# A two-layer hybrid decoder on eight cores: first transfers in the order of use, compact gate weights, the first blocks run k by k, sample tokens moved to the last tile, a scheduler that counts table loads exactly

## The chip, the cores and the metric

The kernel runs as one program on all eight cores of one Trainium2 chip, two dies of four cores. The metric is the device time in microseconds (us) of the slowest core. Each core works alone: it takes one prompt sequence of 2048 tokens and 16 sample sequences of 4 tokens, and reads all weights itself.

Runs come in two states. In the slow state the cores of one die show a lower granted TensorE clock, and the time is up to some 18% longer, whatever the kernel; such runs are left out everywhere below. The runs were made on several chips, and the chips differ by up to 0.8 per cent in fast runs too, so an experiment is always compared with runs of the kernel before on the same chip, in the same rounds.

## The reference

Each of two layers does the following (cut to what matters):

```python
hn = _rmsnorm(x, norm_in)
z  = hn @ w_in                        # 1024 -> 8 x 1024
u_a, b_a, c_a, g_a, x_b, g_b, m_a, m_b = split(z)
y_a = b_a * conv3(c_a * u_a) * silu(g_a)               # branch A
xc  = conv4(x_b) + bias                                # branch B
r   = sigmoid(xc @ blockdiag(w_r) + b_r)               # 16 blocks of 64 x 64
gi  = sigmoid(xc @ blockdiag(w_i) + b_i)
a   = exp(-8 * r * softplus(-lam))
h_t = a_t * h_(t-1) + sqrt(1 - a_t**2) * gi_t * xc_t   # a scan over time
y_b = h * silu(g_b)
x   = x + (sigmoid(m_a) * (y_a @ w_a_out) + sigmoid(m_b) * (y_b @ w_b_out)) @ w_o
x   = x + (p[l] @ w_pe) * sigmoid(_rmsnorm(x) @ w_pg)
```

A final RMSNorm follows. The prompt starts from zero states; the samples start from given convolution and recurrent states. The outputs are y and the new states of both.

## The kernel before

The 2112 tokens of a core are cut into five tiles of 424 columns (the last has 416), in two groups: tiles 0 and 1, then tiles 2, 3 and 4. For each group and layer an *A phase* makes the branches: eight units j of 128 channels, and for each tile six *blocks* of eight matmuls with weights w_A, two *gate matmuls* (the 64 x 64 blocks, two to a 128 x 128 matrix) and the elementwise work. A *B phase* merges them, with weights w_M, w_O and w_G. The B phase of one group runs interleaved with the A phase of the next; so there are five stages, and only stage 0 (A phase of two tiles) and the last (B phase of three) have TensorE work of one kind.

The order is not written by hand. The kernel states each operation with its reads, writes, a priority and an estimated duration for each engine that may do it. A list scheduler then fixes the buffers, the engine and the order of every instruction. On the chip each engine runs its list strictly in that order, waiting on semaphores where data come from another engine.

The parts (cuts marked):

```python
SETS = {"tanh": ("exp", "silu"), "exp": ("exp", "lnexp"), "silu": ("silu",), ...}
WIN, WIN_W = 45.0, 30.0
...
def schedule(self):
    ...
    for o in cand[e]:
        if o.prio > head[o.stream] + o.look and o.prio < 1e6:
            continue
        ...
        s = max(T, o.ready, a)             # T: engine free, ready: inputs, a: buffers
        key = o.prio
        if e == "act" and o.aset and cur[0] not in self.SETS[o.aset]:
            key += 4.0
        k2 = (max(s - T, 0.0) > 0.02, s if s > T + 0.02 else 0.0, key, o.idx)
    ...
    if e == "act" and o.aset and cur[0] not in self.SETS[o.aset]:
        s += SW                            # 1.3 us, an ACT table load
        cur[0] = self.SETS[o.aset][0]
    ...
    for q in o.succ:
        q.ready = max(q.ready, o.fin if o.dma is not None
                      else s + dur + self.LAT[e][q.engs[0][0]])
```

```python
def setup_late():                          # after tile 1's x in the order of the text
    st_load(sA[:], scaT, st_sA); st_load(sBs[:], scbT, st_sB); st_load(sH[:], shT, st_sH)
    ...
    for wsrc, wdst, v in ((w_r, wrbd, st_wrbd), (w_i, wibd, st_wibd)):
        ...                                # 64-column pieces straight into the block diagonal
    ...                                    # scalars from lam, b_r, b_i

def norm(t, xs, gcol, prio, final=False):
    ...                                    # squares (ACT, POOL or DVE), 8 sums with `ones` on PE,
    ...                                    # Ln and Exp on ACT, then 8 products on DVE

def group_mm(w, ring, off, src, n, kk, prio, gate=False, after=None):
    bk = Val("bank", "ps")
    def fn(e, en):
        for k in range(kk):                # one operation: waits for all of src
            ins = e.matmul(out=ps(bk, 0, n), lhsT=ring[w.phys][:, off + k * 128:off + (k + 1) * 128],
                           rhs=b16(src[k // 2], a, a + n), start=(k == 0), stop=(k == kk - 1))
        return ins
    G.op([("pe", d_mm(n, kk))], fn, [w] + src[:kk // 2], [bk], prio, gate=gate, ...)

ns = NS if t == 0 else 0                   # the 64 sample tokens stand in tile 0

bzr = Val("bank", "zr")                    # the gate matmuls; xcb is the bf16 cast of xc
G2(0.3, [("pe", d_mm(n, 1))], lambda e, en: e.matmul(out=ps(bzr, 0, n), lhsT=wrbd[:, l, j, :],
                 rhs=b16(xcb, 0, n), start=True, stop=True), [xcb, st_wrbd], [bzr], gate=True)

for g in range(2):                         # first transfers
    for ti, t in enumerate(GROUPS[g]):
        pr = (-900.0 + 100 * ti) if g == 0 else stage_t[1] - 22.0 + 5 * ti
        x0 = load_x(t, xin, pr, res=0 if g == 0 else 12)
        hn[g, ti] = norm(t, x0, V_NIN, pr + 5.0)
    if g == 0:
        setup_late()
```

Of the kernel before, what the change touches and what calls it, by code (L numbers as in the profile page):

```python
# [5 lines left out]
F32 = mybir.dt.float32  # L6
BF16 = mybir.dt.bfloat16
AF = mybir.ActivationFunctionType
ALU = mybir.AluOpType
# [17 lines left out]
PSPLIT = TN[0] - NS  # L27
# [19 lines left out]
DV_EPS = 64  # L47
# [28 lines left out]
class Graph:  # L76
# [7 lines left out]
    SETS = {"tanh": ("exp", "silu"), "exp": ("exp", "lnexp"), "silu": ("silu",), "sqrt": ("sqrt",), "ln": ("lnexp",)}  # L84


    WIN, WIN_W = 45.0, 30.0
# [5 lines left out]
    def op(self, engs, fn, R, W, prio, aset=None, dma=None, gate=False, after=()):  # L93
# [5 lines left out]
        o.look = self.WIN if dma is None else self.WIN_W if dma[0] in ("d_ra", "d_rb") else 0.0  # L99
        o.stream, o.done = self.stream, False  # L100
# [36 lines left out]
    def schedule(self):  # L137
# [10 lines left out]
        cur = [None]  # L148
# [44 lines left out]
        while n_left:  # L193
            best = None
            for e in ENG:
                T = free[e]
                eb = None
                for o in cand[e]:
                    if o.prio > head[o.stream] + o.look and o.prio < 1e6:
                        continue  # L200
# [3 lines left out]
                    s = max(T, o.ready, a)  # L204
                    key = o.prio
                    if e == "act" and o.aset and cur[0] not in self.SETS[o.aset]:
                        key += 4.0
# [5 lines left out]
                    k2 = (max(s - T, 0.0) > 0.02, s if s > T + 0.02 else 0.0, key, o.idx)  # L213
# [9 lines left out]
            if e == "act" and o.aset and cur[0] not in self.SETS[o.aset]:  # L223
                s += SW
                cur[0] = self.SETS[o.aset][0]
# [19 lines left out]
            for q in o.succ:  # L245
                q.npred -= 1
                q.ready = max(q.ready, o.fin if o.dma is not None else s + dur + self.LAT[e][q.engs[0][0]])
                if q.npred == 0:
                    for x, _ in q.engs:
                        cand[x].append(q)  # L250
# [84 lines left out]
def build_nc():  # L335
# [18 lines left out]
    w_r = din("w_r", [L, 16, 64, 64])  # L354
    w_i = din("w_i", [L, 16, 64, 64])
# [8 lines left out]
    with ExitStack() as ctx:  # L364
        def sb(name, shape, dt):
# [8 lines left out]
        dv = sb("dv", [128, NDV], F32)  # L374
        sA = sb("sA", [128, L, KC, SB, 2], F32)
# [8 lines left out]
            + [f"d_b{i}" for i in range(NBUF)] + ["d_vecs", "d_sA", "d_sB", "d_sH", "d_wr", "d_wi"] + [f"d_pt{i}" for i in range(len(TN))] + [ "d_so0", "d_so1"]  # L384
# [45 lines left out]
        st_vecs, st_dv, st_sA, st_sB, st_sH = (Val("static", s, s) for s in ("vecs", "dv", "sA", "sB", "sH"))  # L430
        st_wrbd, st_wibd, st_ones = (Val("static", s, s) for s in ("wrbd", "wibd", "ones"))
# [7 lines left out]
        G.op([("sp", 0.1)], [lambda e: e.dma_start(out=vecs[:], in_=vecs_d)], [], [st_vecs], PR0, dma=("d_vecs", 0.2, None, 0))  # L439

        def st_load(dst, src, v):
            G.op([("sp", 0.1)], [lambda e: e.dma_start(out=dst, in_=src)], [], [v], -400.0, dma=("d_" + v.name, 0.5, None, 0))

        G.op([("pool", 0.2)], lambda e, en: e.memset(ones[:], 1.0 / D), [], [st_ones], PR0)
        G.op([("pool", 0.2)], lambda e, en: e.memset(dv[:, DV_EPS:DV_EPS + 1], EPS), [], [st_dv], PR0)
        G.op([("pool", 0.2)], lambda e, en: e.memset(dv[:, DV_QTR:DV_QTR + 1], 0.25), [], [st_dv], PR0)

        def setup_late():
            st_load(sA[:], scaT, st_sA)
            st_load(sBs[:], scbT, st_sB)  # L450
            st_load(sH[:], shT, st_sH)
            PR = -300.0
            G.op([("pool", 1.8)], lambda e, en: e.memset(wrbd[:], 0.0), [], [st_wrbd], PR)
            G.op([("pool", 1.8)], lambda e, en: e.memset(wibd[:], 0.0), [], [st_wibd], PR)
            for wsrc, wdst, v in ((w_r, wrbd, st_wrbd), (w_i, wibd, st_wibd)):
                fns = []
                for l in range(L):
                    for half in range(2):
                        src = wsrc[l].rearrange("(j h) i o -> h i j o", h=2)[half]
                        dst = wdst[half * 64:(half + 1) * 64, l, :, half * 64:(half + 1) * 64]  # L460
# [589 lines left out]
```

## Time and profile before

| | kernel before |
|---|---|
| time, median of the first 3 runs (lowest to highest) | 1572.34 us (1570.21 to 1573.26) |
| busy share of TensorE (PE), VectorE (DVE), ScalarE (ACT), GpSimd (POOL) | 95, 70, 67, 21% |
| matmuls; one warm 424-column matmul, start to start | 8200; 0.179 us |

PE is the bound: 8200 matmuls at 0.179 us are 1468 us of a span of 1569.5. What can be won lies in the other 102 us. These are lines of the page of the kernel before: the span, PE's busy time, the DMA packets and the chain of waits that ended last, by engine.

```profile
span 1569.5 us, 23924 instructions; the slowest of 8 cores (1560.4 to 1569.5 us)
...
PE 1486.7 (95%) x8200; PEld 804.3 (51%) x8200; DVE 1098.7 (70%) x1991; ACT 1053.9 (67%) x1535; POOL 323.3 (21%) x690
...
DMA packets 68981, 151.99 MB, mean 97 GB/s; under 512 B 11392, under 2 KB 39808, under 8 KB 68864
...
PE 85%; ACT 5%; DVE 4%; DMA 3%; issue 2%; POOL 1%; SPq 0%; DVEq 0%; ACTq 0%; POOLq 0%
```

The table of windows of core 4 cuts the span into stretches. A row has the bounds and length of the stretch, the busy time of each engine with its instructions in brackets, the mean clock and the DMA share. The window's length minus its matmuls times 0.179 us is what PE lost there.

```profile
core 4: us, PE busy (x) PEld busy (x) DVE busy (x) ACT busy (x) POOL busy (x), PEclk, DMA share, GB/s
0.00:55.70 55.70, 20.68 (x72) 8.27 (x73) 12.85 (x28) 19.95 (x30) 14.15 (x36) 0.94 0.78 145
55.70:124.00 68.30, 68.30 (x383) 37.32 (x382) 54.39 (x116) 59.65 (x91) 24.27 (x61) 1.00 0.49 78
124.00:214.00 90.00, 80.80 (x427) 42.00 (x425) 73.94 (x154) 83.24 (x123) 25.86 (x71) 0.96 0.64 113
214.00:280.00 66.00, 59.78 (x311) 30.95 (x312) 59.85 (x104) 50.84 (x70) 22.32 (x31) 0.95 0.50 101
280.00:1540.00 1260.00, 1248.24 (x6967) 681.38 (x6967) 879.01 (x1560) 827.08 (x1207) 236.75 (x492) 1.00 0.49 92
...
```

So PE lost 42.8 us before 55.7 us, nothing in the next stretch, 13.6 and 10.3 us in the two after it, and 12.9 us in the 1260 us that follow. The timeline of core 4 (start, length, engine, line, what it did, and in brackets how long the engine was idle and what ended it):

```profile
5.05 0.56 ACT L528 ACTIVATE buf<-buf 128x424 bf16<-128x424 f32 x1 [2.70 <-DMA buf<-xin]
...
10.96 0.56 ACT L528 ACTIVATE buf<-buf 128x424 bf16<-128x424 f32 x1 [5.35 <-DMA buf<-xin]
...
28.31 4.66 DVE L550 SCALAR_TENSOR_TENSOR buf<-buf,vecs_sb 128x424 bf16<-128x424 f32 x8 [28.31 <-ACT buf L540]
...
33.11 5.09 PE L562 MATMUL ps<-buf,wb 128*128 128x424 bf16 x16 [6.27 <-DVE buf L550]
...
48.82 7.19 PE L562 MATMUL ps<-buf,wb 128*128 128x424 bf16 x24 [5.50 <-DVE dv L471]
```

The pieces of tile 0's x land between four w_M weights that nothing needs yet: its squares (L528) run at 5.05 and 10.96 us and so on. The first block of matmuls waits for all eight products (L550) and starts at 33.1 us. Another stop of 5.5 us follows behind tile 1's norm.

### The profile page before, as it was taken

The numbers are of one execution on the slowest core, as the hardware profiler recorded it, in microseconds if no ns is written. First come the engines' busy times: TensorE is split into PE (matmuls) and PEld (weight loads), VectorE is DVE, ScalarE is ACT, GpSimd is POOL, SyncE is SP. The second block draws the span as 40 slices with busy tenths as digits, with TensorE's granted clock in tenths as the row PEclk, the third lists the DMA queues.
The fourth block names the chain that finished last, engine by engine and source line by source line (L and its number), as shares of the span: only waits on it lengthen the run. The fifth ranks groups of instructions, "written<-read, shape, count | busy, mean of one in ns | idle before, by whom it ended". The sixth has DMA issues, their size and how long they took to land.

```text
span 1569.5 us, 23924 instructions; the slowest of 8 cores (1560.4 to 1569.5 us)
## 1 busy us (share of the span) xinstructions
PE 1486.7 (95%) x8200; PEld 804.3 (51%) x8200; DVE 1098.7 (70%) x1991; ACT 1053.9 (67%) x1535; POOL 323.3 (21%) x690
## 2 busy tenths in 40 slices
PE   2898989999999999999999999999999999999994
PEld 0454445555555555555555555555555555555542
DVE  1587898776677988556667898766668899333486
ACT  2699987987587787366456777778767778111354
POOL 3133232221122322111112231111112231000100
PEclk9999999999999999999999999999999999999997
DMA  9356654444635374444374478524464525553423
GB/s 190 56 82 91 129 120 92 79 82 79 151 59 89 77 153 69 80 76 85 63 177 65 78 141 181 80 47 80 75 154 72 85 50 135 130 104 66 71 48 133
DMA packets 68981, 151.99 MB, mean 97 GB/s; under 512 B 11392, under 2 KB 39808, under 8 KB 68864
## 3 DMA queue, kind: packets, MB, share of 16 engines
q0 software_dynamic: 39200, 105.46, 41.3%
q1 hardware_dynamic: 29664, 45.00, 9.5%
q8 instruction: 69, 1.13, 0.3%
q14 instruction: 48, 0.39, 0.1%
HBM read 237.74 MB, written 18.14 MB: 163 GB/s over the span
## 4 chain that ended last, share of the span: by engine, by line
PE 85%; ACT 5%; DVE 4%; DMA 3%; issue 2%; POOL 1%; SPq 0%; DVEq 0%; ACTq 0%; POOLq 0%
PE ps L562 81%; PE ps L534 2%; DVE buf L550 1%; DMA buf<-xin 1%; DMA wa<-w_A 1%; PE ps L705 1%; DVE buf L546 1%; PE ps L708 1%; DVE buf L630 1%; ACT L713 0%; ACT L721 0%; ACT buf L717 0%; ACT buf L713 0%; ACT buf L719 0%; DMA wb<-w_O 0%
## 5 line engine op out<-in xcount | busy, mean ns | idle before, releaser
L562 PE MATMUL ps<-buf,wb 128*128 128x424 bf16 (+1 forms) x4000 | 745.9, 344 | 16.4 <-DVE buf L550 9.0
L562 PE MATMUL ps<-buf,wa 128*128 128x424 bf16 (+1 forms) x3840 | 716.8, 343 | 8.2 <-DMA wa<-w_A 5.8
L562 PEld LDWEIGHTS ps<-buf,wb 128*128 128x128 bf16 x4000 | 393.0, 98 | 345.7 <-issue 28.8
L562 PEld LDWEIGHTS ps<-buf,wa 128*128 128x128 bf16 x3840 | 376.4, 98 | 322.0 <-issue 16.4
L798 DVE SCALAR_TENSOR_TENSOR buf<-buf,ps 128x424 f32<-128x424 f32 (+1 forms) x160 | 94.5, 592 | 215.1 <-PE ps L562 176.8
L796 ACT ACTIVATE buf<-ps 128x424 f32<-128x424 f32 (+1 forms) x160 | 81.3, 517 | 152.1 <-PE ps L562 150.4
L630 DVE SCALAR_TENSOR_TENSOR buf<-buf,vecs_sb 128x424 f32<-128x424 f32 (+2 forms) x240 | 153.9, 641 | 3.4 <-ACT buf L621 0.7
L550 DVE SCALAR_TENSOR_TENSOR buf<-buf,vecs_sb 128x424 bf16<-128x424 f32 (+1 forms) x160 | 94.9, 665 | 40.9 <-ACT buf L540 40.6
L686 DVE SCALAR_TENSOR_TENSOR buf<-buf,vecs_sb 128x424 f32<-128x424 f32 (+2 forms) x160 | 106.7, 667 | 2.9
L528 ACT ACTIVATE buf<-buf 128x424 bf16<-128x424 f32 (+1 forms) x98 | 53.0, 553 | 79.7 <-DVE buf L814 39.9
L721 ACT ACT_TABLE_LOAD x80 | 102.6, 1283 | 1.4
L534 PE MATMUL ps<-buf,ones 128*128 128x424 bf16 (+1 forms) x200 | 52.4, 353 | 37.2 <-ACT buf L528 27.6
L717 ACT ACT_TABLE_LOAD x63 | 80.8, 1283 | 1.1
L605 ACT ACTIVATE buf<-ps 128x360 f32<-128x360 f32 (+2 forms) x80 | 40.4, 505 | 55.2 <-PE ps L562 54.9
L814 DVE SCALAR_TENSOR_TENSOR buf<-ps,buf 128x424 f32<-128x424 f32 (+1 forms) x80 | 47.7, 596 | 39.2 <-PE ps L562 38.8
L503 POOL DMA_DIRECT2D wb<-w_M x64 | 35.0, 547 | 192.9 <-PE ps L562 189.7
L752 ACT ACTIVATE buf<-ps 128x424 f32<-128x424 f32 (+1 forms) x80 | 41.6, 520 | 47.5 <-PE ps L562 42.1
L723 DVE SCALAR_TENSOR_TENSOR buf<-buf 128x424 f32<-128x424 f32 (+1 forms) x80 | 49.9, 623 | 27.4 <-ACT buf L715 27.4
L725 DVE TENSOR_TENSOR buf<-buf 128x424 f32<-128x424 f32 (+1 forms) x78 | 47.7, 611 | 30.2 <-ACT buf L721 29.9
L695 ACT ACT_TABLE_LOAD x46 | 59.0, 1283 | 11.4 <-PE ps L562 10.7
L835 ACT ACTIVATE buf<-ps 128x424 f32<-128x424 f32 (+1 forms) x80 | 40.4, 517 | 36.2 <-PE ps L562 35.9
L695 ACT ACTIVATE buf<-ps 128x424 f32<-128x424 f32 (+1 forms) x80 | 41.8, 522 | 33.8 <-PE ps L562 28.8
(92 smaller groups left out, 1531.3 us busy)
## 6 DMA issues: line engine op xcount, KB each, us to landing
wa<-w_A POOLq DMA_DIRECT2D x96, 512.0 KB, 7.4
wb<-w_M POOLq DMA_DIRECT2D x64, 512.0 KB, 6.5
buf<-xin SPq DMA_DIRECT2D x64, 212.0 KB, 9.1
wb<-w_G POOLq DMA_DIRECT2D x32, 320.0 KB, 4.8
wb<-w_O POOLq DMA_DIRECT2D x32, 256.0 KB, 5.2
xsp<-buf SPq DMA_DIRECT2D x32, 212.0 KB, 6.2
buf<-xsp SPq DMA_DIRECT2D x32, 212.0 KB, 6.6
yT<-buf SPq DMA_DIRECT2D x32, 212.0 KB, 2.6
```

Source lines behind the costliest of these rows:

```text
L528: return e.activation(out=b16(h, a, a + n), in_=f32(x, 0, n), func=AF.Square)
L534: G.op([("pe", d_mm(n, 1))], lambda e, en, h=h, a=a, k=k: e.matmul(out=ps(bk, 0, n), lhsT=ones[:], rhs=b16(h, a, a + n), start=(k == 0), s ...
L550: G.op([("dve", d_sttp(n))], lambda e, en, x=xs[k], h=h, a=a, k=k: e.scalar_tensor_tensor(out=b16(h, a, a + n), in0=f32(x, 0, n), scalar=v ...
L562: ins = e.matmul(out=ps(bk, 0, n), lhsT=ring[w.phys][:, off + k * 128:off + (k + 1) * 128], rhs=b16(src[k // 2], a, a + n), start=(k == 0) ...
L630: G2(0.1 + 0.01 * d, [("dve", d_sttp(npr))], lambda e, en, d=d: e.scalar_tensor_tensor(out=f32(xc, 0, npr), in0=f32(xb, 3 - d, 3 - d + npr ...
L686: G2(1.3 + 0.01 * d, [("dve", d_sttp(npr))], lambda e, en, d=d: e.scalar_tensor_tensor(out=f32(cv, 0, npr), in0=f32(cu, d, d + npr), scala ...
L695: G2(1.5, [("act", d_act(n))], lambda e, en: e.activation(out=f32(tg, 0, n), in_=ps(bga, 0, n), func=AF.Silu), [bga], [tg], aset="silu")
L717: G2(0.5, [("act", d_act(n, 2))], lambda e, en: e.activation(out=f32(av, 0, n), in_=f32(tr, 0, n), func=AF.Exp, bias=dcol(DV_CH + lj), sca ...
L721: G2(0.6, [("act", d_act(n, 1))], lambda e, en: e.activation(out=f32(tr, 0, n), in_=f32(tr, 0, n), func=AF.Sqrt, bias=dcol(DV_QTR), scale= ...
L723: G2(0.6, [("dve", d_stt(n))], lambda e, en: e.scalar_tensor_tensor(out=f32(tq, 0, n), in0=f32(tq, 0, n), scalar=1.0, in1=f32(xc, 0, n), o ...
L796: G.op([("act", d_act(n))], lambda e, en, q=q, bm=bm, n=n: e.activation(out=f32(q, 0, n), in_=ps(bm, 0, n), func=AF.Tanh, scale=0.5), [bm] ...
L798: G.op([("dve", d_stt(n))], lambda e, en, q=q, bp=bp, n=n: e.scalar_tensor_tensor(out=f32(q, 0, n), in0=f32(q, 0, n), scalar=1.0, in1=ps(b ...
```

## The change

Its intent: load first what is used first (tile 0's x, then w_A, w_r and w_i, tile 1's x; states and the second layer's gate weights later); load the gate weights in one compact piece per matrix and layer, and spread them into the block diagonal on DVE; run the first unit's blocks as eight single matmuls, so that each waits for its own piece of the norm; do three of the eight products of the first norms on ACT and POOL (`split`); move the sample tokens from tile 0, whose stage 0 has the most elementwise work per matmul, to the last tile. The scheduler counts ACT table loads exactly (the set of tables that may be loaded, instead of one guess), limits how far one stream may run ahead (`WIN_B`), exempts the first operations (priority below 0) from the older limit, and lets a weight load follow the issue of the load before it, no longer its landing.

The diff, cut to its core:

```diff
-    SETS = {"tanh": ("exp", "silu"), "exp": ("exp", "lnexp"), ...}
-    WIN, WIN_W = 45.0, 30.0
+    SETS = {f: frozenset(v) for f, v in {...}.items()}
+    WIN, WIN_W, WIN_B = 45.0, 30.0, 100.0
 ...
+        if prio < 0:
+            o.look = 1e9
 ...
-                    if o.prio > head[o.stream] + o.look and o.prio < 1e6:
+                    if o.prio < 1e6 and (o.prio > head[o.stream] + o.look or o.prio > head[0] + self.WIN_B):
 ...
-                    if e == "act" and o.aset and cur[0] not in self.SETS[o.aset]:
+                    if e == "act" and o.aset and not cur[0] & self.SETS[o.aset]:
+                        s = max(T + SW, o.ready, a)
                         key += 4.0
 ...
-            if e == "act" and o.aset and cur[0] not in self.SETS[o.aset]:
-                s += SW
-                cur[0] = self.SETS[o.aset][0]
+            if e == "act" and o.aset:
+                cur[0] = (cur[0] & self.SETS[o.aset]) or self.SETS[o.aset]
 ...
-                q.ready = max(q.ready, o.fin if o.dma is not None else ...)
+                q.ready = max(q.ready, (s + dur if q.dma is not None and q.dma[0] == o.dma[0] and o.dma[0] in ("d_ra", "d_rb") else o.fin)
+                              if o.dma is not None else ...)
 ...
+        def setup_gates(l, prio, behind=()):
+            for i, (dst, v) in enumerate(((wrbd, st_wrbd[l]), (wibd, st_wibd[l]))):
+                ...memset...; c = Val("buf", "wc")
+                G.op([("pool", 0.55)], [...dma_start(out=b16(c, 0, KC * 64), in_=w_ri[l, i])], list(behind), [c], prio, ...)
+                for h in range(2):
+                    G.op([("dve", 0.35)], ...tensor_copy(out=dst[q, l, :, q], in_=b16(c, 0, KC * 64)[q]...), [c], [v], prio)
 ...
-        def norm(t, xs, gcol, prio, final=False):
+        def norm(t, xs, gcol, prio, final=False, split=()):
+            for k in split:
+                G.op([("act", d_act(n, 1))], ...activation(out=gx[k], in_=xs[k], func=AF.Copy, scale=vcol(gcol + k))...)
 ...
+                if k in gx:
+                    G.op([("pool", d_ptt(n))], ...tensor_tensor(in0=gx[k], in1=rs, op=ALU.mult)...)
 ...
+            if fine:
+                for k in range(kk):
+                    G.op([("pe", d_mm(n, 1))], ...one matmul..., [w, (src[k // 2], k % 2)], [bk], prio)
+                return bk
 ...
-            ns = NS if t == 0 else 0
+            ns = NS if t == len(TN) - 1 else 0
 ...
-                return group_mm(w, ring, o, hn, n, KC, p0 + off)
+                return group_mm(w, ring, o, hn, n, KC, p0 + off, fine=l == 0 and g == 0 and j == 0)
 ...
-                W = [load_w("ra", w_A[l, j, i], 2048, S + Ln * done / tot - 20.0 + 2 * i) for i in range(3)]
+                W = [load_w("ra", w_A[l, j, i], 2048, -41.0 + 10 * i if start else S + Ln * done / tot - 20.0 + 2 * i,
+                            behind=(first_x[3:4] if i == 0 else first_x[7:8]) if start else ()) for i in range(3)]
 ...
-                pr = (-900.0 + 100 * ti) if g == 0 else stage_t[1] - 22.0 + 5 * ti
-                x0 = load_x(t, xin, pr, res=0 if g == 0 else 12)
-                hn[g, ti] = norm(t, x0, V_NIN, pr + 5.0)
-            if g == 0:
-                setup_late()
+                pr = (-43.0 + 14 * ti) if g == 0 else stage_t[1] - 22.0 + 5 * ti
+                x0 = load_x(t, xin, pr, res=0 if g == 0 else 12, behind=first_x[7:8] if g == 0 else ())
+                ...setup_vecs(-44.0); setup_gates(0, -33.0, x0[7:8]); setup_gates(1, 40.0); setup_states(60.0, x0[7:8])...
+                hn[g, ti] = norm(t, x0, V_NIN, pr + (1.0 if g == 0 else 5.0), split=(2, 5, 7) if g == 0 else ())
 ...
-        toks = np.concatenate([xp[:PSPLIT], xs, xp[PSPLIT:]], axis=0)
+        toks = np.concatenate([xp, xs], axis=0)
```

## The prediction

> **What bounds it now.** The page has 8200 matmuls; in the timeline a warm 424-column one issues every 0.179 us, so TensorE needs about 1467 of the 1569.5 us. The table of windows (window minus matmuls times 0.179 us) splits the other 102 us: about 35 before 55.7 us, 24 from 55.7 to 280 us, 14 from 280 to 1545 us, the rest in the tail. The change aims at the first and may touch the second.
>
> **The start, from the timeline.** Four w_M weights are issued first (1.6 to 3.9 us), though nothing needs them before the first norm. Tile 0's x lands behind them: first piece at 5.05 us, second at 10.96, eighth at about 25.6. The normalized tile is made from 28.3 to 33.0; the first block waits for all eight pieces and starts at 33.1. It runs cold: weight loads 0.353 us apart instead of 0.179, as the Trainium skill's "TensorE: Matmul & The Clock Gate", Part 1, says of an idle array. Twelve w_M blocks fill until 55.7, with a second stop of 5.5 us behind tile 1's norm. Only then do w_A blocks begin; the second and third w_A are issued at 36.9 and 61.5 us, because POOL sat 22.1 us behind the sample states (L608). The gate weights (64 KB, 22 to 25 us to landing, against 6 to 7 for a 512 KB weight) make nearly all of the 4736 packets under 512 B.
>
> **After, costed.** From the queue table: 3.3 us of all engines per x MB, 3.2 us per 512 KB weight. Tile 0's x: 5.8 us, landed by about 10 us; with squares, sums, Ln, Exp the first matmul is at about 13 us (was 33). Three w_A of j=0 land at 14 to 20 us, tile 1's x by 25, w_A of j=1 by 37 (estimate: the sum of these transfers). By 37 us TensorE has done two units (17.9 us) and norms, about what it had done by 55.7. Gain about 16 us; k by k is perhaps 3 of it, compact gate weights perhaps 5, the rest is order.
>
> **Middle.** Sample side operations leave stage 0 (56 to 214 us), where ACT is 92% and DVE 81% busy: by the groups, 17 us of small DVE work less about 4 for wider tiles. They go to the stages with three tiles, where TensorE is 99% and DVE 75% busy: nearly free. The w_M filler, no longer spent at the start, is left for 124 to 234 us, where 23 us are lost to late w_A (5.8), cold restarts and group 1's norms. I expect about 9 us back, the least certain term. The scheduler's new accounting of ACT tables (320 loads of 1.28 us) may move things either way. Tail: unchanged within 5 us.
>
> **Prediction: 1547 us (-25, 1.6%)**, 8 in 10 between 1534 and 1561. Faster by over 2% 0.28, within 2% 0.71, slower 0.01.
>
> **What would show it.** First matmul at 11 to 16 us; w_A blocks first, no w_M before about 50 us; far fewer packets under 512 B; 64-column operations gone from stage 0; TensorE's loss before 280 us down from 59 to about 34 us, after 280 us within 5 of 36.
>
> **What would make it wrong.** w_A of j=1 later than 37 us, with a second cold stop; ACT bounding stage 0 without filler, so that the start's gain is waited for later; POOL, in order, holding weight issues behind a late operation; the tail reordered by the scheduler. If stage 0 loses nearly nothing, it goes over 2%.

## More of the kernel before

One more view matters later: the waits of PE in the stretch from 44 to 1540 us, core 4 (what waited, for what; us in total, times, longest). These are the lines of the gate matmuls L705.

```profile
PE ps L705 <- POOL buf L642: 5.5, 3, 2.7
...
PE ps L705 <- ACT buf L641: 2.9, 3, 1.3
PE ps L705 <- DVE buf L697: 1.3, 1, 1.3
```

About 10 us, mostly for the bf16 cast of xc, a copy in the narrower type that the gate matmul reads (L641 on ACT, L642 on POOL).

## The result, and the profile after

| | before | after |
|---|---|---|
| median of 4 fast runs (lowest to highest) | 1571.28 us (1570.02 to 1573.26) | 1575.33 us (1573.75 to 1577.53) |
| ratio of fast runs, 95% interval | | 1.0026 (1.0008 to 1.0043) |

A ratio here and below compares one kernel's fast runs with the other's of the same rounds, so it is not quite the ratio of the medians quoted. The change predicted to win 25 us lost 4. The same lines of the page, of the kernel after:

```profile
span 1573.4 us, 23995 instructions; the slowest of 8 cores (1568.9 to 1573.4 us)
...
PE 1489.9 (95%) x8200; PEld 803.1 (51%) x8200; DVE 1102.5 (70%) x1984; ACT 1076.5 (68%) x1565; POOL 344.6 (22%) x687
...
DMA packets 65765, 151.99 MB, mean 97 GB/s; under 512 B 7280, under 2 KB 36848, under 8 KB 65648
...
PE 70%; DVE 12%; ACT 11%; issue 3%; DMA 2%; POOL 1%; SPq 0%; DVEq 0%; ACTq 0%; POOLq 0%
```

The small packets went as intended. But the chain that ended last now runs through DVE and ACT for 23% of the span, 9% before, which points to PE waiting for them more. The slowest core, whose page this is, is core 2; core 4 is shown from here on, as before, since its span (1569.6 us) is that of the kernel before to a tenth. The same windows of core 4 after:

```profile
0.00:55.70 55.70, 25.77 (x99) 10.48 (x100) 27.06 (x49) 24.96 (x40) 19.50 (x33) 0.85 0.69 133
55.70:124.00 68.30, 65.22 (x364) 35.28 (x362) 51.99 (x92) 66.07 (x86) 21.76 (x46) 1.00 0.73 115
124.00:214.00 90.00, 79.25 (x424) 41.10 (x423) 74.50 (x119) 85.75 (x116) 32.70 (x54) 0.98 0.61 125
214.00:280.00 66.00, 63.09 (x349) 33.58 (x347) 60.19 (x112) 52.36 (x76) 18.52 (x39) 1.00 0.47 81
280.00:1540.00 1260.00, 1242.52 (x6924) 677.11 (x6923) 870.11 (x1585) 833.90 (x1232) 250.61 (x517) 1.00 0.48 91
...
```

By the same sum PE lost 38.0, 3.1, 14.1, 3.5 and 20.6 us, together 79.3, which is to a tenth what the five stretches lost before (42.8 - 0.3 + 13.6 + 10.3 + 12.9). The start won 4.8 us where 16 were expected, and the long stretch after 280 us gave back 7.7.

Why did the start win so little? The timeline of core 4 after (SPq is SyncE's queue, which issues x; x8 are the eight pieces of tile 1):

```profile
11.56 4.72 SPq L519 DMA_DIRECT2D buf<-xin  x8
...
14.18 6.39 DVE L564 SCALAR_TENSOR_TENSOR buf<-buf,vecs_sb 128x424 bf16<-128x424 f32 x5 [2.65 <-ACT buf L551]
14.66 3.16 POOL L557 TENSOR_TENSOR buf<-buf 128x424 bf16<-128x424 f32 x3
...
18.44 2.99 PE L582 MATMUL ps<-buf,wa 128*128 128x424 bf16 x8 [5.66 <-DVE buf L564]
...
27.32 0.34 PE L540 MATMUL ps<-buf,ones 128*128 128x424 bf16 x1 [3.66 <-DVE buf L535]
...
31.41 0.51 PE L540 MATMUL ps<-buf,ones 128*128 128x424 bf16 x1 [3.74 <-DVE buf L535]
...
34.88 0.51 PE L540 MATMUL ps<-buf,ones 128*128 128x424 bf16 x1 [2.96 <-DVE buf L535]
...
```

The first block starts at 18.4 us instead of 33.1: the order of the first transfers does what it should. But from 23.7 to 41.8 us PE does next to nothing except five norm sums (L540), most of them 3 to 4 us apart, and two gate matmuls. Each of these sums waits for a square, and each square for a piece of tile 1's x. The pieces were issued from 11.6 to 16.3 us and landed at 17.3, 18.9, 21.7, 26.5, 30.6, 34.0, 36.9 and 37.3 us (the DMA view), while w_A and gate weights issued from POOL landed in between. PE's list is in order, so tile 0's blocks that stand behind tile 1's sums cannot pass, although the second and third w_A, which they need beside tile 0's norm, had landed at 26.1 and 30.2 us.

How the lead of the kernel after moved is seen from the start time of the nth matmul (counted from 0, so 8 is the first after tile 0's norm sums), core 4 against core 4:

| matmul | 8 | 50 | 100 | 1400 | 2800 | 3000 | 4700 | 4800 | 5800 | 6800 | last |
|---|---|---|---|---|---|---|---|---|---|---|---|
| lead, us | 14.7 | 2.5 | 5.0 | 11.9 | 11.0 | 6.5 | 6.1 | 1.6 | 0.0 | -1.6 | 1.4 |

The lead is not lost evenly but in steps. One lies at 583 us, as the timeline of core 4 after shows:

```profile
579.25 3.51 DVE L564 SCALAR_TENSOR_TENSOR buf<-buf,vecs_sb 128x424 bf16<-128x424 f32 x6
579.46 3.68 POOL L663 CAST buf<-buf 128x416 bf16<-128x416 f32 x1 [7.61 <-DVE buf L655]
...
583.39 0.34 PE L726 MATMUL ps<-buf,wrbd 128*128 128x416 bf16 x1 [3.41 <-POOL buf L625]
```

A cast on POOL took 3.68 us, where the 24 others of this core took 0.5 to 1.3, for as long as six DVE products of a norm ran, and the gate matmul L726 behind it held PE for 3.4 us. (The profile names POOL L625, a tiny copy that follows the cast; the releaser is inferred, and the cast just before it is what took the time.) The waits of PE from 44 to 1540 us, core 4 after, the largest of the gate matmuls:

```profile
PE ps L726 <- ACT buf L662: 7.0, 8, 2.8
PE ps L726 <- POOL buf L663: 6.7, 5, 2.5
...
PE ps L726 <- POOL buf L625: 3.4, 1, 3.4
PE ps L726 <- POOL buf L622: 2.6, 1, 2.6
...
```

These four are 19.7 us of the 26.7 on L726, where all gate waits before were about 10.

### A budget

To compare versions over all eight cores, I split each core's span by its matmul records and took the mean of the cores of the profiled run. "Start" is the time to the 101st matmul. A "stop" is a gap between consecutive starts that exceeds 0.179 us by over 0.12 us more than a lower clock explains; it is put down to the matmul that follows: gate, norm sum or block. "Mid" ends at matmul 7990, the tail follows. "Slow clock" is the loss of unstopped matmuls under a granted clock below full: half (cold), or 13/16.

| us | before | after | difference |
|---|---|---|---|
| start | 60.7 | 56.1 | -4.6 |
| 8100 matmuls at 0.17917 | 1451.3 | 1451.3 | |
| slow clock (cold only) | 7.2 | 5.4 | -1.8 |
| gate stops, mid | 11.6 | 31.0 | +19.4 |
| norm stops, mid | 5.7 | 1.7 | -4.0 |
| block stops, mid | 12.7 | 9.0 | -3.7 |
| stops in the tail | 10.4 | 8.5 | -1.9 |
| after the last matmul | 11.5 | 13.0 | +1.5 |
| rest (missing records, rounding) | -5.4 | -5.1 | +0.3 |
| span, mean of cores | 1565.8 | 1570.9 | +5.1 |

So two questions: why is the start's gain 5 and not 16 us, and where do 19 us of gate stops come from?

### The profile page after: what moved, and what is told of

It is laid out like the page before. It is cut to its first block, busy times and chain, and to the rows that moved or that the text cites. A ratio compares the mean times of both kernels' runs of the same rounds, so it can differ in the third digit from the quotient of the medians.

```text
span 1573.4 us, 23995 instructions; the slowest of 8 cores (1568.9 to 1573.4 us)
## 1 busy us (share of the span) xinstructions
PE 1489.9 (95%) x8200; PEld 803.1 (51%) x8200; DVE 1102.5 (70%) x1984; ACT 1076.5 (68%) x1565; POOL 344.6 (22%) x687
## 2 busy tenths in 40 slices
DMA packets 65765, 151.99 MB, mean 97 GB/s; under 512 B 7280, under 2 KB 36848, under 8 KB 65648
## 4 chain that ended last, share of the span: by engine, by line
PE 70%; DVE 12%; ACT 11%; issue 3%; DMA 2%; POOL 1%; SPq 0%; DVEq 0%; ACTq 0%; POOLq 0%
PE ps L576 66%; DVE buf L564 2%; DVE buf L651 2%; DMA buf<-xin 2%; ACT L742 1%; PE ps L540 1%; DVE buf L860 1%; ACT L738 1%; DVE buf L862 1%; PE ps L582 1%; PE ps L726 1%; ACT L740 1%; ACT buf L738 1%; DVE buf L560 1%; DVE buf L707 1%
## 5 line engine op out<-in xcount | busy, mean ns | idle before, releaser
L576 PE MATMUL ps<-buf,wa 128*128 128x424 bf16 (+1 forms) x3744 | 695.8, 342 | 1.5 <-DVE buf L564 1.2
L576 PEld LDWEIGHTS ps<-buf,wb 128*128 128x128 bf16 x4000 | 392.3, 98 | 333.0 <-issue 15.8
L576 PEld LDWEIGHTS ps<-buf,wa 128*128 128x128 bf16 x3744 | 366.3, 98 | 304.4 <-issue 5.7
L651 DVE SCALAR_TENSOR_TENSOR buf<-buf,vecs_sb 128x424 f32<-128x424 f32 (+1 forms) x240 | 156.3, 651 | 6.6 <-ACT buf L642 3.8
L534 ACT ACTIVATE buf<-buf 128x424 bf16<-128x424 f32 (+1 forms) x111 | 60.8, 551 | 90.0 <-DVE buf L837 47.8
L707 DVE SCALAR_TENSOR_TENSOR buf<-buf,vecs_sb 128x424 f32<-128x424 f32 (+1 forms) x160 | 105.5, 659 | 2.4
L564 DVE SCALAR_TENSOR_TENSOR buf<-buf,vecs_sb 128x424 bf16<-128x424 f32 (+1 forms) x154 | 97.2, 701 | 4.9 <-ACT buf L551 3.5
L540 PE MATMUL ps<-buf,ones 128*128 128x424 bf16 (+1 forms) x200 | 52.7, 356 | 29.2 <-ACT buf L534 10.9
L626 ACT ACTIVATE buf<-ps 128x424 f32<-128x424 f32 (+1 forms) x80 | 40.5, 506 | 54.2 <-PE ps L576 52.4
L734 ACT ACTIVATE buf<-ps,dv 128x424 f32<-128x424 f32 (+1 forms) x80 | 48.9, 611 | 24.3 <-PE ps L726 22.3
L716 ACT ACTIVATE buf<-ps 128x424 f32<-128x424 f32 (+1 forms) x80 | 41.8, 522 | 32.8 <-PE ps L576 32.4
L509 POOL DMA_DIRECT2D wa<-w_A x96 | 52.5, 551 | 45.6 <-PE ps L576 29.6
```

The lines of the kernel that those rows point to most:

```text
L509: fn = lambda e: e.dma_start(out=ring[v.phys][:, 0:cols], in_=src)
L534: return e.activation(out=b16(h, a, a + n), in_=f32(x, 0, n), func=AF.Square)
L540: G.op([("pe", d_mm(n, 1))], lambda e, en, h=h, a=a, k=k: e.matmul(out=ps(bk, 0, n), lhsT=ones[:], rhs=b16(h, a, a + n), start=(k == 0), s ...
L564: G.op([("dve", d_sttp(n))], lambda e, en, x=xs[k], h=h, a=a, k=k: e.scalar_tensor_tensor(out=b16(h, a, a + n), in0=f32(x, 0, n), scalar=v ...
L651: G2(0.1 + 0.01 * d, [("dve", d_sttp(npr))], lambda e, en, d=d: e.scalar_tensor_tensor(out=f32(xc, 0, npr), in0=f32(xb, 3 - d, 3 - d + npr ...
L707: G2(1.3 + 0.01 * d, [("dve", d_sttp(npr))], lambda e, en, d=d: e.scalar_tensor_tensor(out=f32(cv, 0, npr), in0=f32(cu, d, d + npr), scala ...
```

## The experiments

Theories of the start: tile 1's x lands late and PE stands behind its norm; or the late x only hides another limit, so that an earlier x wins little. Theories of the middle: the schedule has become too tight, so that any overrun of a cast stops PE (then slack removes the stops from any version); or the sample operations, now in the stages with three tiles, fill ACT and DVE (then moving them back removes them); or the new limit `WIN_B` reordered the streams (then lifting it does); or POOL and DVE hinder each other (then taking work from POOL does). Edits of the scheduler reorder the whole program, so part of each result is luck of the order; where I could I made the same edit on both kernels. Where the clock was lower, stops were a little smaller (28.5 against 31.0 us for the same kernel on two chips); that operands had more time there is likely but not shown. Edits that do not aim at the gate stops moved them from 28.5 to between 20.7 and 27.5 us, so a single difference below some 8 us is not read as an effect.

All sixteen kernels gave correct results. The table has the ratio to the kernel before on the same chip (95% interval), the medians of fast runs of both, and the lines of the budget, in us. Four kernels each ran on one chip, in the order of the table's four parts. "Gate" and "norm + block" are the stops in mid, "end" the time after the last matmul. "Slow clock" is cold and 13/16 together: the chips of the first, second and fourth part show stretches at 13/16 in fast runs too; the chip of the third part, and that of the runs above, show none.

| kernel | ratio (interval) | this / before | start | gate | norm + block | end | slow clock |
|---|---|---|---|---|---|---|---|
| u_x1first | 0.9978 (0.9958 to 0.9998) | 1579.11 / 1582.92 | 44.8 | 20.7 | 15.8 | 12.4 | 22.6 |
| u_told | 0.9931 (0.9916 to 0.9947) | 1572.24 / 1582.92 | 51.9 | 21.9 | 5.6 | 12.8 | 18.1 |
| u_nosplit | 0.9991 (0.9973 to 1.0009) | 1582.90 / 1582.92 | 51.9 | 25.8 | 10.2 | 12.7 | 21.4 |
| u_sfirst | 1.0059 (1.0036 to 1.0082) | 1592.43 / 1582.92 | 56.2 | 11.2 | 20.9 | 12.4 | 27.2 |
| k_after | 1.0027 (1.0005 to 1.0049) | 1585.03 / 1580.35 | 55.8 | 28.5 | 11.5 | 12.9 | 12.2 |
| b_slast | 1.0003 (0.9990 to 1.0015) | 1579.94 / 1580.35 | 60.4 | 14.4 | 19.7 | 11.9 | 9.0 |
| b_graph | 0.9963 (0.9949 to 0.9976) | 1573.58 / 1580.35 | 53.7 | 14.3 | 17.1 | 12.1 | 14.6 |
| t_slack2 | 0.9931 (0.9912 to 0.9951) | 1570.43 / 1580.35 | 49.6 | 3.0 | 21.0 | 17.6 | 14.0 |
| a_winb | 0.9993 (0.9980 to 1.0006) | 1569.79 / 1570.89 | 55.5 | 27.5 | 6.5 | 13.0 | 5.7 |
| a_bgraph | 1.0008 (0.9976 to 1.0041) | 1570.24 / 1570.89 | 56.3 | 17.1 | 16.8 | 13.0 | 5.4 |
| b_slack2 | 0.9942 (0.9895 to 0.9988) | 1558.34 / 1570.89 | 58.8 | 0.0 | 19.0 | 21.3 | 4.7 |
| c_best2 | 0.9889 (0.9875 to 0.9903) | 1553.27 / 1570.89 | 46.3 | 2.6 | 23.0 | 17.8 | 4.5 |
| x_oldtab | 0.9972 (0.9952 to 0.9992) | 1576.39 / 1579.12 | 55.8 | 15.3 | 14.1 | 13.1 | 10.2 |
| x_nopool | 0.9962 (0.9929 to 0.9996) | 1570.13 / 1579.12 | 55.7 | 6.6 | 18.5 | 12.1 | 11.5 |
| u_nofine | 0.9905 (0.9889 to 0.9921) | 1564.54 / 1579.12 | 52.4 | 22.8 | 6.1 | 12.8 | 8.8 |
| c_best7 | 0.9875 (0.9854 to 0.9897) | 1560.26 / 1579.12 | 46.0 | 2.0 | 19.8 | 15.6 | 12.9 |

The kernel after, run again as k_after, shows the same ratio and the same stops on another chip; its start, gate stops and ratio (55.8, 28.5, 1.0027) are what the edits of the kernel after are held against.

### u_x1first: w_A after tile 1's x

```diff
-  behind=(first_x[3:4] if i == 0 else first_x[7:8]) if start else ()
+  behind=(first_x[3:4] if i == 0 else second_x[7:8]) if start else ()     # second_x: tile 1's x
```

> The kernel after, with one wait changed: the second and third w_A of the first block are issued once the last x piece of tile 1 has landed, not of tile 0; that is the order in which the list scheduler's model lets them land. Theory A (the start's gain was lost because tile 1's x shared the DMA engines with w_A and landed at 17 to 37 us where the fixed order assumed 12 to 18, and TensorE, VectorE and ScalarE stood in order behind it): x of tile 1 lands by about 21 us, TensorE's stop of 16 us from 25 to 41 us shrinks to under 6, matmul 100 starts 8 to 13 us earlier than in the kernel after (at 43 to 48 us instead of 56), and as the order is fixed and no engine is full later, most of it stays: 1562 to 1567 us. Rival B (stage 0 is bound by ACT and DVE, so the lead is waited for later): matmul 100 earlier, but matmul 1000 at 235 to 238 us as in the kernel after, time 1573 to 1577.

Tile 1's x landed between 16.4 and 23.7 us (core 4), not between 17.3 and 37.3, and the 101st matmul comes 11 us earlier (44.8 instead of 55.8), as the late-x theory has it. Of these 11 us the time kept about 8 (0.5% of 1580): block stops in mid rose from 9.8 to 13.2 us and cold time from 5.7 to 8.7, while gate stops fell. The absolute time expected did not come, as this chip is slower for both kernels.

### u_told: the scheduler told when these transfers really land

```diff
 # cut: nm is the name of the tile that the transfer fills
+  if o.prio < 0:
+      o.fin += {"x1.0": 5.0, "x1.1": 5.8, "x1.2": 8.0, "x1.3": 12.0, "x1.4": 16.0,
+                "x1.5": 18.3, "x1.6": 19.8, "x1.7": 19.5, "ra": 5.0}.get(nm, 0.0)
```

No transfer's condition is edited; only the schedule's belief of when tile 1's pieces and the first w_A land is set to what the trace showed.

> The kernel after; the scheduler's model alone is told the measured landing times of tile 1's x and the first w_A (5 to 20 us later), no transfer is moved and no operation added. Theory A: the four other blocks of tile 0 are run while tile 1's x comes; matmul 100 starts 4 to 7 us earlier than 56 us, time 1568 to 1572. Rival B: within 1 us of the kernel after, 1574 to 1577. If transfers alone bound the start (C), matmul 100 also stays at 54 us or later.

The start shortens by 4 us, and the whole by almost 1% (0.9931 against 1.0027), more than expected. Tile 1's x still lands almost as late (by 36.0 instead of 37.3 us on core 4), but 27 block matmuls now run from 30.3 to 36.4 us, in front of its last norm sums. Gate stops and norm + block stops fall by about 6 us each; whether that comes of the landings or of the new order is open.

### u_nosplit: all eight products on DVE

```diff
-  hn[g, ti] = norm(t, x0, V_NIN, pr + (1.0 if g == 0 else 5.0), split=(2, 5, 7) if g == 0 else ())
+  hn[g, ti] = norm(t, x0, V_NIN, pr + (1.0 if g == 0 else 5.0), split=())
```

> The kernel after without the split of the first norms (no copies on ACT, no products on POOL; all eight pieces on DVE as before). The first DVE product took 4.11 us in the kernel after, while three POOL products ran, instead of 0.65. If POOL holds DVE off: no first product over 1 us, the first w_A matmul at 15 to 17 us instead of 18.4. As tile 1's x still lands at 37 us, theory A expects little at the end: 1572 to 1576 us.

In the kernel after, the first DVE product (L564) took 4.11 us, from 14.18 to 18.29, while the three POOL products (L557, 1.1 us each) ran; the other four of this tile took 0.65. Without the split all took 0.65, and the first block started at 15.89 instead of 18.44 us: sharing this work with POOL delayed it. The Trainium skill, "SBUF — State Buffer", section "Who interferes with whom", says that a DVE instruction with two SBUF inputs contends with a GpSimd instruction that reads SBUF; the 4.11 us agree. The time gained 0.4%, near the noise: the interval overlaps that of k_after.

### u_sfirst: samples back in tile 0

```diff
-  ns = NS if t == len(TN) - 1 else 0
+  ns = NS if t == 0 else 0
-  setup_states(60.0, x0[7:8])
+  setup_states(-28.0, x0[7:8])          # and the token order, in and out, as before
```

> The kernel after with the sample tokens back in the first tile (their states loaded early, as that tile needs them). Theory M (the lead is given back in the middle because the sample tile's longer chain makes gate matmuls wait in the stages with three tiles: 4.5 us near 583 us, 4.5 near 915, 2.5 from 1000 to 1100): those stops go, the lead over the kernel before at matmul 3000 is kept, and stage 0 pays 3 to 6 us; time 1566 to 1571. Rival R (any change of the list order moves stops of 2 to 4 us about, whatever the samples do): other stops of the same sum, time 1573 to 1582.

The gate stops fall from 28.5 to 11.2 us, so the place of the samples matters for them. Norm and block stops rise by 9.4 us, all of it in stage 0, before the 1000th matmul, where 3 to 6 had been expected. Stops taken together, the edit saves 8 us. Yet the kernel is slower, and that lies in the clock: its fast runs had a mean granted clock of 0.969, the kernel before on the same chip 0.979, and its slow-clock time is 6 us above that of u_nosplit on that chip and 15 above that of k_after on another. Whether this order draws more or it was chance, no run tells; so the ratio of this run says little about the samples.

### k_after and b_slast: the kernel after again, and the samples alone

```diff
 # k_after: no edit.   b_slast, in the kernel before:
-  ns = NS if t == 0 else 0
+  ns = NS if t == len(TN) - 1 else 0     # and the token order, in and out
```

> The kernel after, unchanged, as the control of this chip: ratio to the kernel before 1.000 to 1.005, as on the first chip (1.0026); its stops behind tile 1's x (16 us) and at 583, 915 and 1289 us at the same instructions.

> The kernel before with the sample tokens moved to the last tile, nothing else. Theory M (the move helps stage 0 and costs stops in the two stages with three tiles): matmul 1000 some 5 us earlier than in the kernel before, 4 to 9 us given back at the last blocks of stages 1 and 3; in sum a ratio of 0.997 to 1.003. If the move is what ate the gain: 1.003 to 1.010. If it is plain gain, as the schedule's model says of the kernel after: 0.990 to 0.996.

The move of the samples alone is worth nothing: 1.0003. Alone it hardly adds gate stops either (14.4 against 11.6), though it moves them: before the 1000th matmul they rise from 1.6 to 8.1 us, after it they fall.

### b_graph and a_bgraph: the two schedulers exchanged

b_graph is the kernel before with the `Graph` class of after; a_bgraph is the kernel after with that of before.

```diff
-class Graph: ...        # SETS of tuples, cur[0] one table, no WIN_B
+class Graph: ...        # SETS of frozensets, cur[0] a set, WIN_B, prio < 0, loads from their issue (b_graph; a_bgraph the other way)
```

> The kernel before with the list scheduler of the kernel after (its table accounting, its limit on how far stage B may run ahead, weight loads counted from their issue), nothing else. The model promises 13 us. If the model's promises are kept outside the start: 0.990 to 0.994. Theory S (the model's promise is not kept, as the fixed order runs as tight as the model and each real delay stops TensorE): 0.997 to 1.004, with the slip between modelled and real start of the last matmul grown by 8 us or more over the 38 us of the kernel before.

> The kernel after with the whole list scheduler of the kernel before, and all else of the change. If the new scheduler together with the moved samples makes the gate stops (28 to 31 us in the kernel after, 14 with either part alone): under 18 us of them, ratio 0.993 to 1.000, although the schedule's model calls it 19 us longer than the kernel after. If the start and the samples are enough: 25 us or more of them, 1.001 or above.

The new scheduler on the old kernel is 0.4% faster, about 6 us where its model promised 13, with 14.3 us of gate stops. The old scheduler on the new kernel lowers the stops from 28.5 to 17.1 us; its ratio is that of the kernel before, but the interval holds 1.0027 as well. Neither part alone makes the 30 us: the samples give 14.4, the scheduler 14.3, both with the rest of the change 28.5 to 31.0.

### t_slack2 and b_slack2: 2 us of slack before each gate and norm-sum matmul

```diff
-  else s + dur + self.LAT[e][q.engs[0][0]]
+  else s + dur + self.LAT[e][q.engs[0][0]] + (2.0 if q.gate and e != "pe" else 0.0)
```

The only edit: the schedule believes that operands made by other engines reach these matmuls 2 us later, so it puts other matmuls in front of them. No wait is added on the chip.

> The kernel after; the scheduler is told that a gate matmul or a norm sum can start only 2 us after its operand is ready, so that other blocks stand before it in TensorE's order; nothing else. The model says 12 us longer. Theory S (the gate matmuls are placed so tight that each late cast or copy stops TensorE): the waits of TensorE at the gate matmuls (18 us in the kernel after) fall under 8 us, ratio to the kernel before 0.993 to 0.999. If the model is right on the order's worth: 1.006 to 1.012.

> The kernel before with 2 us of slack before gate matmuls and norm sums in the schedule's model, nothing else. Its gate stops are 11.6 us and its stops at norm sums 5.7 us in the middle. Theory S (slack removes stops in whichever kernel): gate stops under 4 us, ratio 0.992 to 0.997, so less than the 1% that it took off the kernel after. If the change is needed for it to pay: 0.998 to 1.003.

On both kernels the gate stops vanish: 28.5 to 3.0 us in the kernel after, 11.6 to 0.0 in the kernel before. So these stops come from operands that are late by less than some 2 us, with too little work in front of the matmul. The gate waits that remain of PE from 44 to 1540 us, core 4 of t_slack2, are:

```profile
PE ps L726 <- ACT buf L662: 2.2, 3, 0.9
...
PE ps L726 <- ACT buf L626: 0.4, 1, 0.4
```

The time gains about 1% (0.9931 against 1.0027), some 15 us, of which 6 are a shorter start (49.6 instead of 55.8). That is less than the stops: norm + block stops rise by 9.5 us, and the end after the last matmul grows from 12.9 to 17.6 us (11.5 to 21.3 in the kernel before), probably since in the tail nothing is left to put in front.

### a_winb: the limit on running ahead lifted

```diff
-  WIN, WIN_W, WIN_B = 45.0, 30.0, 100.0
+  WIN, WIN_W, WIN_B = 45.0, 30.0, 1e9
```

> The kernel after without the new limit that keeps stage B's work within 100 us of stage A's head, nothing else. In the kernel after, TensorE stops 11 us at gate matmuls in stage 0 (matmuls 100 to 1000; 1.6 us in the kernel before). Theory W (with the limit stage 0 has no w_M blocks to put between a cast and its gate matmul): those 11 us fall under 5, ratio to the kernel before 0.995 to 1.000. Rival G (the new accounting of tables and of loads makes the order tight by itself): they stay at 8 us or more, ratio 1.001 to 1.006.

The gate stops stay at 27.5 us: the theory of `WIN_B` fell. The ratio, 0.9993, is lower than its rival had it too (1.001 to 1.006).

### x_oldtab and x_nopool: two parts that may make the order tight

```diff
 # x_oldtab: only the table accounting of before, in the kernel after
-  if e == "act" and o.aset and not cur[0] & self.SETS[o.aset]:
-      s = max(T + SW, o.ready, a)
+  if e == "act" and o.aset and cur[0] not in self.SETS[o.aset]:
 ...
 # x_nopool: POOL taken out of the choices for squares, casts, three products and the merge's add
-  G2(0.2, [("act", d_act(n)), ("pool", d_pcp(n)), ("dve", d_ts(n))], fc, [xc], [xcb])
+  G2(0.2, [("act", d_act(n)), ("dve", d_ts(n))], fc, [xc], [xcb])
```

> The kernel after with the old accounting of ACT's tables alone (the counting of the model and the choice that it makes). If the new accounting makes the order tight: gate stops under 20 us (28 in the kernel after, 17.1 with the whole old scheduler), ratio 0.996 to 1.001. If not: 24 us or more, ratio within 0.3% of the kernel after's 1.0027, and what is left is the counting of weight loads and transfers from their issue.

> The kernel after with POOL taken out of the choice for squares, casts and products (small copies and memsets stay; the split of the first norms stays). Theory L (the delays come from POOL and DVE holding each other off): DVE's back-to-back excess over the model falls from 68 us to under 40, gate stops from 28 to under 16 us, ratio 0.993 to 0.999. If the tight order stops at any delay whatever its source: gate stops 22 us or more, ratio 0.999 to 1.008, as DVE has more to do.

With the old accounting the gate stops fall to 15.3 us. The old scheduler charged the kernel before for 350 table loads, of which the chip made 320; the new one charges 328 for the kernel after, and 328 are made. The 30 loads that never came, 1.3 us each, were slack that nobody had meant to give. Of the 15.3 us, 10.3 lie before the 1000th matmul, as many as in k_after (10.6); what fell are the later ones (17.7 to 5.0). With POOL out of the choices the gate stops fall to 6.6 us. DVE's back-to-back instructions then took 46 us in all more than the schedule's formulas give, against 68 in the kernel after (under 40 had been expected); so a third of the overruns is tied to POOL's work, as in the cast of 3.68 us, but not all. Both edits also made a looser list (counted under "Why the prediction was wrong", point 3), so their fall of stops is not the work of one cause alone.

### u_nofine: the first unit's blocks whole again

```diff
-  return group_mm(w, ring, o, hn, n, KC, p0 + off, fine=l == 0 and g == 0 and j == 0)
+  return group_mm(w, ring, o, hn, n, KC, p0 + off)
```

> The kernel after with the first blocks run whole, not k by k. The prediction gave k by k 3 us. In the kernel after the first block starts at 18.4 us and tile 1's x holds everything up from 25 us, so I expect matmul 100 within 2 us of 55.8 us and a ratio within 0.4% of 1.0027, by the luck of the order; matmul 100 later by 3 us or more would show a worth.

A miss: I expected hardly any change, and the kernel is 1.2% faster without it (0.9905 against 1.0027). The start is 3.4 us shorter, gate stops fall by 5.7 us, norm + block stops by 5.4. What is shown is that k by k does not help here; how much of the 1.2% is its own cost and how much luck of a new order is open. The scheduler's own reckoning had it 7 us shorter without k by k (1500 against 1507).

### c_best2 and c_best7: what helped, together

c_best2 is the kernel after with the edits of u_x1first, u_nosplit and t_slack2. c_best7 gives the slack only to operations of priority below 1390, so not in the tail.

```diff
-  else s + dur + self.LAT[e][q.engs[0][0]]
+  else s + dur + self.LAT[e][q.engs[0][0]] + (2.0 if q.gate and e != "pe" and q.prio < 1390.0 else 0.0)
 # and split=(), and w_A behind second_x[7:8]
```

> The kernel after with three mends together: w_A of the first block behind tile 1's x, no split of the first norms, 2 us of slack. If the gains add (start 9 us earlier than 55.8 us at matmul 100, gate stops under 5 us): the budget's sum without limited clock at 1540 to 1548 us, ratio to the kernel before 0.983 to 0.990. If the start's gain is waited for in stage 0 by ACT (rival B): as with slack alone, 0.992 to 0.995.

> The mended kernel (w_A behind tile 1's x, no split, 2 us of slack) without the slack for the last norms. The time from the last matmul to the end was 17.8 us with it and 12.9 without: expected 12 to 14 us, stops at the last norms 8 to 10 instead of 6.5, ratio 0.985 to 0.989 against 0.9889.

Both beat both kernels: 0.9889 and 0.9875, about 1.2% below the kernel before. The intervals overlap, so the two are not told apart, nor is c_best2 from u_nofine alone (0.9889 to 0.9921); all of these edits together were not run. The end is 15.6 us in c_best7, where 12 to 14 had been expected. The start of c_best7, in the timeline of core 4:

```profile
16.61 2.99 PE L582 MATMUL ps<-buf,wa 128*128 128x424 bf16 x8 [4.52 <-DVE buf L564]
...
31.25 14.98 PE L582 MATMUL ps<-buf,wa 128*128 128x424 bf16 x75
```

Tile 1's norm is over by 31 us instead of 42, and 75 matmuls follow without a stop. The gate waits of PE from 44 to 1540 us on this core are one line:

```profile
PE ps L726 <- ACT buf L662: 1.6, 2, 0.9
```

## Why the prediction was wrong

1. **The start, predicted at 16 us, was 4.6.** The step that failed is "tile 1's x by 25, w_A of j=1 by 37 (estimate: the sum of these transfers)", with "by 37 us TensorE has done two units". I added the transfers up as if they came one after the other in the order of use. In the trace, x from SP's queue and weights from POOL's queue shared the engines, and tile 1's x landed at 37.3 us, after w_A. The Trainium skill, "DMA: Bandwidth & Descriptors", section "Issuing engines are not separate DMA queues", says that transfers started by different engines run on the same 16 engines and interleave; this trace agrees, with pieces that took 5.8 to 21.8 us to land. Four of the last five pieces landed 0.1 to 0.4 us after one w_A each (26.5 after 26.1, 30.6 after 30.2, 34.0 after 33.7, 36.9 after 36.8 us), so a piece of 212 KB came at the pace of the 512 KB beside it, which a sum in the order of use leaves out. I also left out that PE, ACT and DVE stand, in order, behind tile 1's norm. Moving w_A behind it gave 11 us back (u_x1first), which is the missing part; with the split gone and slack as well the start is 46.0 us (c_best7), 14.7 below the kernel before, so the gain of some 16 us was there and the overlap of the transfers was what I had mis-sized. The first block was predicted at 13 us and came at 18.4, after the 11 to 16 that I had named as a sign; of that, 2.5 us were the split over POOL, to which I had given no cost (u_nosplit). Without the split it started at 15.89 us, 0.3 us after the first w_A landed (15.6): my 13 us had left that weight out, though the same sum lets w_A land at 14.

2. **"About 35 us" lost before 55.7 us was misread.** The window minus its 72 matmuls is 42.8 us. I also wrote of twelve w_M blocks; the 72 are 16 norm sums and seven blocks. The reading made the start look closer to full than it was, but did not change the sign of anything.

3. **The middle, predicted at 9 us back, gave about 10 away** (gate stops +19.4, norm stops -4.0, block stops -3.7, cold time -1.8: together +9.9). The step that failed is that sample operations moved to stages where DVE is 75% busy are "nearly free", with "about 9 us back". I reasoned from mean busy shares. A busy share says nothing about a single operand that comes late in an in-order list. The samples alone are in fact free (b_slast 1.0003), and so is the new scheduler alone (b_graph 0.9963); together with the rest they leave an order in which gate matmuls stand directly behind their casts. Slack removes the stops in both kernels (3.0 and 0.0 us left), and the lists themselves show the tightness. Each kernel has 80 first gate matmuls, one for each unit and tile. Called tight here are those that the schedule starts within 0.3 us of the moment at which its model has their operand ready:

   | version | tight, of 80 | gate stops, us |
   |---|---|---|
   | before | 18 | 11.6 |
   | samples alone (b_slast), scheduler alone (b_graph) | 15, 12 | 14.4, 14.3 |
   | after with the old scheduler (a_bgraph), with the samples back (u_sfirst) | 16, 12 | 17.1, 11.2 |
   | x_oldtab, x_nopool | 21, 19 | 15.3, 6.6 |
   | after, and the five other edits of it without slack | 31 to 36 | 20.7 to 31.0 |
   | the four versions with slack | 0 | 0.0 to 3.0 |

   The stops go with this count. The operands also came later on the chip: one cast in ten ran over 2.0 us later against PE than the model has it in the kernel after, over 0.8 before (core 4); but t_slack2 bears casts just as late (2.5). Half of the 19.4 us lies before the 1000th matmul, in the stage that the samples left, the other half later (from 10.0 to 19.3). That the old table accounting was hidden slack is shown in part, as restoring it in the kernel after removes about half the stops (15.3 left), while introducing the new one in the kernel before adds only 2.7 us (b_graph). Why only the parts together give so tight a list is open.

4. **k by k, predicted at plus 3 us of gain, costs.** Without it the kernel is 1.2% faster (u_nofine); the share of luck in this is open.

5. **What else came, as predicted or not.** The w_A blocks come first, no w_M runs before about 198 us, packets under 512 B fell from 11392 to 7280, the 64-column operations left stage 0, the first block came far earlier (18.4 against 33.1 us), and the tail stayed within 5 us (stops 10.4 to 8.5, end 11.5 to 13.0). TensorE's loss before 280 us fell from 66.4 to 58.7 us on core 4, where it was to fall to 34, and after 280 us it grew by 7.7, where it was to stay within 5. The matmuls after an idle stretch ran at half clock, 0.353 us apart, which is what the Trainium skill's "TensorE: Matmul & The Clock Gate", Part 1, says and the prediction used. Of the named risks a second stop came, though behind tile 1's x and not behind w_A of j=1 (its first piece landed at 33.7 us); and stage 0 did give the start's gain back in part, as gate stops up to the 1000th matmul went from 1.6 to 11.7 us.

The size to learn from: the scheduler's own reckoning, made as the kernel is built, ended at 1530 us before and 1507 us after. It promised 23 us, much as I did, and with the same two assumptions: transfers that land when the sum says, and operations that take their usual time. The chip ran 39 us over the first reckoning and 62 us over the second (core 4).

## What to carry to other kernels

When engines run fixed lists in order, a schedule that is shorter and tighter by its own model need not be faster on the chip: give the matmuls that wait on another engine some slack, except where nothing can be put in front, and read the gain from the stops. For the first transfers, order the issue by waiting for what must land first, not by priority alone, because queues share the engines; then put the true landing times into the model. Judge a part of a change by undoing it alone in each kernel, for parts that are harmless alone can cost together.

## What the Trainium skill lacked or had wrong

- "TensorE: Matmul & The Clock Gate", Part 1, section "Seeing it yourself", says that a peak-current limiter takes a die to 13/16 clock within 5 to 20 us of a third core's dense matmuls and holds it while the load lasts. In the fast runs here all eight cores kept TensorE 95% busy for 1570 us; the profiled runs of before, after and the third part of the table show no 13/16 clock at all, those of the other three parts only stretches of some 4 to 15 us at a time, which cost 4 to 24 us of a span (means of the eight cores). Only in slow runs did a die's mean clock come down to that (0.811 to 0.814 in the last run of u_x1first; 13/16 is 0.8125). So what the page gives as the rule for all cores looks here like the slow state; no slow run was traced.
- "SBUF — State Buffer", section "Summary: rules for kernel authors", says that of a DVE and a GpSimd instruction in conflict the second to issue blocks until the first finishes. Here the one that lost waited through a run of several: one DVE product took 4.11 us beside three POOL products of 1.1 us each, and one POOL cast took 3.68 us, until just after a run of six DVE products (579.25 to 582.76 us). Nor was it the second in the first case: by the trace, whose times for POOL are rough, the DVE product started at 14.18 us and POOL's first at 14.66. The page could say so.
- "DMA: Bandwidth & Descriptors" says that transfers of different issuers interleave but gives no landing times for two streams of unlike pieces. Here eight x pieces of 212 KB, issued from SP by 16.3 us, needed until 37.3 us beside w_A weights of 512 KB issued from POOL between 13 and 24 us, and four of the last five landed in step with one weight each.
- I found no page that tells of stops from an in-order list that is too tight: 28.5 us of gate stops went to 3.0 with 2 us of slack in the schedule alone.
